# Instance normalization on one core: engine programs of its own with a loop on the chip, and the last tile in two halves

## The chip, the core and the metric

The kernel runs on one core of a Trainium2 chip. The metric is the device time of one execution in microseconds (us), lower is better. A kernel is run several times and the median is quoted. The profile is one execution taken by the hardware profiler; its span is some 1.7 us shorter than the time quoted. Engine names: PE multiplies matrices, DVE is the vector engine, ACT the scalar engine, POOL is GpSimd, SP issues the loads.

## The reference, cut to what matters

```python
# x: (8, 64, 32, 64, 64) float32, so 512 instances of 131,072 numbers
mean = np.mean(x, axis=(2, 3, 4), keepdims=True)
var = np.var(x, axis=(2, 3, 4), keepdims=True)
return ((x - mean) / np.sqrt(var + eps)).astype(np.float32)
```

Every number is read once and written once: 268.4 MB each way, 536.9 MB in all. There are two passes of arithmetic over each instance before its first number can be written.

## The kernel before

A tile is 128 partitions by 8,192 numbers (4 MB) and holds 8 instances of 16 partitions each; there are 64 tiles in six buffers. The framework of the kernel (its tile pools and scheduler) places all semaphores and waits, and the 64 tiles are written out one after the other in the program of each engine.

```python
avg = singles.tile([P, P], fp32, name="avg")     # 1/n_elem in 16 x 16 blocks: sums over an instance's partitions
...
def load(g):
    t = data_pool.tile([P, F], fp32, name="xt")  # one of six slots
    nc.sync.dma_start(out=t, in_=x_t[g])
    return t

def compute(t):
    cut = F // 2
    sums = stat_pool.tile([P, 2], fp32, name="sums")
    nc.vector.reduce_sum(out=sums[:, 0:1], in_=t[:, :cut], ...)                        # L83
    nc.scalar.activation(out=unused[:, cut:], in_=t[:, cut:], func=Act.Identity,
                         accum_out=sums[:, 1:2])                                       # L86
    nc.tensor.matmul(out=mean_ps, lhsT=avg, rhs=sums, ...)
    nc.vector.tensor_reduce(out=neg_mean, in_=mean_ps, op=Alu.add, negate=True, ...)
    nc.scalar.activation(out=unused, in_=t, func=Act.Square, bias=neg_mean,
                         accum_out=squares)                                            # L103
    nc.tensor.matmul(out=var_ps, lhsT=avg, rhs=squares, ...)
    ...   # std, 1/std, bias: four small instructions
    nc.vector.tensor_scalar(out=t[:, cut:], in0=t[:, cut:], scalar1=scale, scalar2=bias, ...)   # L114
    nc.scalar.activation(out=t[:, :cut], in_=t[:, :cut], func=Act.Identity,
                         scale=scale, bias=bias)                                       # L122

for g in range(n_tiles):
    t = load(g)
    compute(t)
    nc.scalar.dma_start(out=out_t[g], in_=t)                                           # L131
```

Of the kernel before, what the change touches and what calls it, by code (L numbers as in the profile page):

```python
# [1 line left out]

# [4 lines left out]


@with_exitstack
def kernel(  # L10
    ctx: ExitStack,
    tc: tile.TileContext,
    x: bass.AP,
    eps: bass.AP,
    out: bass.AP,
):
    nc = tc.nc
    fp32 = mybir.dt.float32
    Alu = mybir.AluOpType
    Act = mybir.ActivationFunctionType  # L20

    P = 128
    B, C, D, H, W = x.shape
    n_inst = B * C
    n_elem = D * H * W
    eps_f = float(eps)

    SPLIT = 16
    IPT = P // SPLIT
    F = n_elem // SPLIT  # L30
    n_tiles = n_inst // IPT
    SLOTS = 6

    x_t = x.rearrange("b c d h w -> (b c) (d h w)").rearrange(
        "(k i) (s f) -> k (i s) f", i=IPT, s=SPLIT
    )
    out_t = out.rearrange("b c d h w -> (b c) (d h w)").rearrange(
        "(k i) (s f) -> k (i s) f", i=IPT, s=SPLIT
    )

    singles = ctx.enter_context(tc.tile_pool(name="singles", bufs=1))
    data_pool = ctx.enter_context(tc.tile_pool(name="data", bufs=SLOTS))
    stat_pool = ctx.enter_context(tc.tile_pool(name="stats", bufs=4))
    psum_pool = ctx.enter_context(
        tc.tile_pool(name="psum", bufs=2, space=bass.MemoryType.PSUM)
    )


    avg = singles.tile([P, P], fp32, name="avg")
    nc.vector.memset(avg, 1.0 / n_elem)  # L50
    nc.gpsimd.affine_select(  # L51
        out=avg,
        in_=avg,
        pattern=[[-SPLIT, IPT], [0, SPLIT]],
        compare_op=Alu.is_ge,
        fill=0.0,
        base=0,
        channel_multiplier=1,
    )
    nc.gpsimd.affine_select(  # L60
        out=avg,
        in_=avg,
        pattern=[[SPLIT, IPT], [0, SPLIT]],
        compare_op=Alu.is_ge,
        fill=0.0,
        base=SPLIT - 1,
        channel_multiplier=-1,
    )

    eps_t = singles.tile([P, 1], fp32, name="eps_t")  # L70
    nc.vector.memset(eps_t, eps_f)  # L71

    unused = singles.tile([P, F], mybir.dt.uint8, name="unused")

    def load(g):
        t = data_pool.tile([P, F], fp32, name="xt")
        nc.sync.dma_start(out=t, in_=x_t[g])
        return t

    def compute(t):  # L80
        cut = F // 2
        sums = stat_pool.tile([P, 2], fp32, name="sums")
        nc.vector.reduce_sum(  # L83
            out=sums[:, 0:1], in_=t[:, :cut], axis=mybir.AxisListType.X
        )
        nc.scalar.activation(  # L86
            out=unused[:, cut:],
            in_=t[:, cut:],
            func=Act.Identity,
            accum_out=sums[:, 1:2],  # L90
        )
        mean_ps = psum_pool.tile([P, 2], fp32, name="mean_ps")
        nc.tensor.matmul(out=mean_ps, lhsT=avg, rhs=sums, start=True, stop=True)  # L93
        neg_mean = stat_pool.tile([P, 1], fp32, name="neg_mean")
        nc.vector.tensor_reduce(  # L95
            out=neg_mean,
            in_=mean_ps,
            axis=mybir.AxisListType.X,
            op=Alu.add,
            negate=True,  # L100
        )
        squares = stat_pool.tile([P, 1], fp32, name="squares")
        nc.scalar.activation(  # L103
            out=unused, in_=t, func=Act.Square, bias=neg_mean, accum_out=squares
        )
        var_ps = psum_pool.tile([P, 1], fp32, name="var_ps")
        nc.tensor.matmul(out=var_ps, lhsT=avg, rhs=squares, start=True, stop=True)  # L107
        std = stat_pool.tile([P, 1], fp32, name="std")
        nc.scalar.activation(out=std, in_=var_ps, func=Act.Sqrt, bias=eps_t)  # L109
        scale = stat_pool.tile([P, 1], fp32, name="scale")  # L110
        nc.vector.reciprocal(out=scale, in_=std)  # L111
        bias = stat_pool.tile([P, 1], fp32, name="bias")
        nc.vector.tensor_mul(out=bias, in0=neg_mean, in1=scale)  # L113
        nc.vector.tensor_scalar(  # L114
            out=t[:, cut:],
            in0=t[:, cut:],
            scalar1=scale,
            scalar2=bias,
            op0=Alu.mult,
            op1=Alu.add,  # L120
        )
        nc.scalar.activation(  # L122
            out=t[:, :cut], in_=t[:, :cut], func=Act.Identity, scale=scale, bias=bias
        )


    with tc.manual_schedule():
        for g in range(n_tiles):
            t = load(g)
            compute(t)  # L130
            nc.scalar.dma_start(out=out_t[g], in_=t)  # L131


# [1 line left out]
_INS = ['x', 'eps']  # L135
_OUTS = [((8, 64, 32, 64, 64), 'float32')]

_NUMBERS = {'eps': 9.999999747378752e-06}


# [26 lines left out]
```

## Time and profile before

| | before |
|---|---|
| time, median of 3 | 1249.35 us (1249.16 to 1250.83) |
| busy: ACT, DVE, PE | 77%, 37%, 6% |
| packets of the load queue and the store queue, share of 16 DMA engines | 49.9% and 49.8% |
| traffic | 430 GB/s |

From the page of the kernel before: the span, each engine's busy time, the DMA row of the 40 slices (busy tenths), and the table of DMA queues (packets, MB, the time of their packets as a share of 16 engines over the span).

```profile
span 1247.6 us, 1828 instructions
PE 73.6 (6%) x256; PEld 64.2 (5%) x256; DVE 467.4 (37%) x322; ACT 961.6 (77%) x386; POOL 0.9 (0%) x6
DMA  9999999999999999999999999999999999999998
...
q1 hardware_dynamic: 9216, 268.44, 49.9%
q10 hardware_dynamic: 9216, 268.44, 49.8%
q14 instruction: 9, 0.07, 0.0%
q8 instruction: 2, 0.03, 0.0%
```

The two data queues together take 99.7% of what 16 DMA engines have, so the DMA bounds the whole span. The two queues of kind "instruction" are easy to pass over, at 0.0%: they bring the program itself.

From the timeline of the kernel before, the last tile (start, duration, engine, line, operation, tiles; in brackets the idle time before it and what ended that):

```profile
1215.30 3.62 ACT L86 ACTIVATE unused<-xt 128x4096 uint8<-128x4096 f32 x1 [1.61 <-DMA xt<-in_x_dram]
...
1220.72 7.12 ACT L103 ACTIVATE unused<-xt,neg_mean 128x8192 uint8<-128x8192 f32 x1 [1.71 <-DVE neg_mean L95]
...
1229.35 3.80 ACT L122 ACTIVATE xt<-xt,bias,scale 128x4096 f32<-128x4096 f32 x1 [0.47 <-DVE bias L113]
1233.18 0.34 ACTq L131 DMA_DIRECT2D out_dram<-xt  x1
```

The last load is there at 1215.3 us, and its store is issued 17.9 us later. It looks as if this stretch stood open, but two earlier stores are still in the queue: the DMA packets show the 16 engines idle for only 0.8 us on average around 1233 us.

### The profile page before, as it was taken

What the parts mean: (1) busy time and instruction counts of PE and PEld (TensorE: products, weight loads), DVE (VectorE), ACT (ScalarE), POOL (GpSimd) and SP (SyncE); (2) the same over time, 40 slices, a digit from 0 to 9 for tenths busy, and PEclk for the clock granted to TensorE, in tenths of its full rate; (3) what the DMA queues carried; (4) which work ended last, traced back from release to release, by engine and by line L of the source; (5) the groups of instructions that cost most, each with busy time, mean ns of one, the idle gap of its engine ahead of it and who ended that gap; (6) DMA issues with size and microseconds to landing.
All of it is one profiled execution on the core that took longest, in us unless ns stands there. A gap on an engine that the chain in (4) does not pass through costs nothing.

```text
span 1247.6 us, 1828 instructions
## 1 busy us (share of the span) xinstructions
PE 73.6 (6%) x256; PEld 64.2 (5%) x256; DVE 467.4 (37%) x322; ACT 961.6 (77%) x386; POOL 0.9 (0%) x6
## 2 busy tenths in 40 slices
PE   0000000000000000000000000000000000000000
PEld 0000000000000000000000000000000000000000
DVE  2344433433334334343343433434334333343331
ACT  5888888787777877778777777777787777877774
POOL 0000000000000000000000000000000000000000
DMA  9999999999999999999999999999999999999998
GB/s 403 420 437 434 434 427 436 435 435 427 435 436 434 434 428 435 435 434 427 437 435 434 433 429 437 435 432 427 437 436 434 429 431 435 436 434 425 437 436 364
DMA packets 18443, 536.99 MB, mean 430 GB/s; under 512 B 2048, under 2 KB 2048, under 8 KB 2048
## 3 DMA queue, kind: packets, MB, share of 16 engines
q1 hardware_dynamic: 9216, 268.44, 49.9%
q10 hardware_dynamic: 9216, 268.44, 49.8%
q14 instruction: 9, 0.07, 0.0%
q8 instruction: 2, 0.03, 0.0%
HBM read 268.44 MB, written 268.44 MB: 430 GB/s over the span
## 4 chain that ended last, share of the span: by engine, by line
ACT 45%; DVE 32%; another core or an unknown queue 12%; PE 6%; issue 2%; DMA 1%; ACTq 0%
ACT unused L103 37%; DVE sums L83 19%; DVE xt L114 10%; ACT xt L122 4%; ACT unused L86 3%; PE var_ps L107 3%; PE mean_ps L93 3%; ACT std L109 1%; DMA xt<-in_x_dram 1%; DVE scale L111 1%; DVE neg_mean L95 1%; DVE bias L113 1%; ACTq L131 0%; ACT L109 0%
## 5 line engine op out<-in xcount | busy, mean ns | idle before, releaser
L103 ACT ACTIVATE unused<-xt,neg_mean 128x8192 uint8<-128x8192 f32 x64 | 455.8, 7121 | 100.6 <-DVE neg_mean L95 100.6
L83 DVE TENSOR_REDUCE sums<-xt 128x1 f32<-128x4096 f32 x64 | 282.8, 4419 | 167.6 <-DMA xt<-in_x_dram 167.6
L86 ACT ACTIVATE unused<-xt 128x4096 uint8<-128x4096 f32 x64 | 231.5, 3617 | 96.1 <-DMA xt<-in_x_dram 91.5
L122 ACT ACTIVATE xt<-xt,bias,scale 128x4096 f32<-128x4096 f32 x64 | 243.3, 3801 | 31.3 <-DVE bias L113 31.3
L111 DVE RECIPROCAL scale<-std 128x1 f32<-128x1 f32 x64 | 10.5, 164 | 530.8 <-ACT std L109 530.8
L114 DVE TENSOR_SCALAR xt<-xt,scale,bias 128x4096 f32<-128x4096 f32 x64 | 154.4, 2413 | 2.7 <-DVE bias L113 0.3
L93 PE MATMUL mean_ps<-sums,avg 128*128 128x2 f32 x128 | 36.0, 351 | 670.9 <-DVE sums L83 573.9
L93 PEld LDWEIGHTS mean_ps<-sums,avg 128*128 128x128 f32 x128 | 32.1, 311 | 674.7 <-ACT unused L86 657.1
L107 PE MATMUL var_ps<-squares,avg 128*128 128x1 f32 x128 | 37.6, 363 | 484.1 <-ACT unused L103 484.1
L107 PEld LDWEIGHTS var_ps<-squares,avg 128*128 128x128 f32 x128 | 32.1, 312 | 489.6 <-ACT unused L103 489.6
L109 ACT ACTIVATE std<-var_ps,eps_t 128x1 f32<-128x1 f32 x64 | 16.7, 261 | 42.7 <-PE var_ps L107 42.7
L95 DVE TENSOR_REDUCE neg_mean<-mean_ps 128x1 f32<-128x2 f32 x64 | 10.2, 160 | 60.1 <-PE mean_ps L93 60.1
L103 ACT ACTIVATION_READ_ACCUMULATOR unused<-xt,neg_mean 128x1 f32 x64 | 11.9, 187 | 0.0
L86 ACT ACTIVATION_READ_ACCUMULATOR unused<-xt 128x1 f32 x64 | 11.9, 186 | 0.0
L113 DVE TENSOR_TENSOR bias<-neg_mean,scale 128x1 f32<-128x1 f32 x64 | 10.2, 160 | 2.2
L86 ACT ACT_TABLE_LOAD x1 | 1.3, 1283 | 0.8 <-PEq L148 0.8
L109 ACT ACT_TABLE_LOAD x1 | 1.3, 1283 | 0.0
L50 DVE MEMSET avg<- 128x128 f32 x1 | 0.2, 165 | 0.9 <-PEq L148 0.9
L51 POOL TENSOR_SCALAR_AFFINE_SELECT avg<-avg 128x128 f32<-128x128 f32 x1 | 0.3, 343 | 0.6 <-DVE eps_t L71 0.6
L60 POOL TENSOR_SCALAR_AFFINE_SELECT avg<-avg 128x128 f32<-128x128 f32 x1 | 0.3, 338 | 0.1
L148 POOL MEMSET const-bfloat16-1.0<- 128x1 bf16 x1 | 0.1, 102 | 0.0
L148 POOL MEMSET const-uint8-127<- 128x1 uint8 x1 | 0.1, 102 | 0.0
(3 smaller groups left out, 0.3 us busy)
## 6 DMA issues: line engine op xcount, KB each, us to landing
xt<-in_x_dram SPq DMA_DIRECT2D x64, 4096.0 KB, 53.3
out_dram<-xt ACTq DMA_DIRECT2D x64, 4096.0 KB, 45.2
```

Source lines behind the costliest of these rows:

```text
L51: nc.gpsimd.affine_select(out=avg, in_=avg, pattern=[[-SPLIT, IPT], [0, SPLIT]], compare_op=Alu.is_ge, fill=0.0, base=0, channel_multiplier=1,
L83: nc.vector.reduce_sum(out=sums[:, 0:1], in_=t[:, :cut], axis=mybir.AxisListType.X)
L86: nc.scalar.activation(out=unused[:, cut:], in_=t[:, cut:], func=Act.Identity, accum_out=sums[:, 1:2],)
L93: nc.tensor.matmul(out=mean_ps, lhsT=avg, rhs=sums, start=True, stop=True)
L95: nc.vector.tensor_reduce(out=neg_mean, in_=mean_ps, axis=mybir.AxisListType.X, op=Alu.add, negate=True,)
L103: nc.scalar.activation(out=unused, in_=t, func=Act.Square, bias=neg_mean, accum_out=squares)
L107: nc.tensor.matmul(out=var_ps, lhsT=avg, rhs=squares, start=True, stop=True)
L109: nc.scalar.activation(out=std, in_=var_ps, func=Act.Sqrt, bias=eps_t)
L111: nc.vector.reciprocal(out=scale, in_=std)
L113: nc.vector.tensor_mul(out=bias, in0=neg_mean, in1=scale)
L114: nc.vector.tensor_scalar(out=t[:, cut:], in0=t[:, cut:], scalar1=scale, scalar2=bias, op0=Alu.mult, op1=Alu.add,)
L122: nc.scalar.activation(out=t[:, :cut], in_=t[:, :cut], func=Act.Identity, scale=scale, bias=bias)
```

## The change

Its intent: replace the framework's scheduling by a program for each engine with semaphores of its own, one set for each slot; put the tiles in a loop on the chip, six to a round, with waits against registers that count up; and cut the last tile in two halves, so that the work after the last load is shorter. The core of the diff, with cuts marked:

```diff
-    with tc.manual_schedule():
-        for g in range(n_tiles):
-            t = load(g)
-            compute(t)
-            nc.scalar.dma_start(out=out_t[g], in_=t)
+    slots = [sbuf(f"slot{s}", [P, COLS]) for s in range(SLOTS)]          # six, as before
+    landed = semaphores("landed", LANES)                                 # and ten more sets
...
+    def on_vector(eng, t, lane, n, c1, c2, c16):
+        eng.reduce_sum(out=a[:, 0:1], in_=t[:, :w], ...
+        )._wait_ge(landed[lane], c16).then_inc(summed[lane], 1)
...  # on_scalar, on_tensor: the same arithmetic and the same split as before
+    rest = [ ... tiles 60 to 62 ... ]
+    for h in range(2):                                                   # last tile: two halves
+        k = 2 * (n_tiles - 1) + h
+        half = slots[last][:, h * COLS // 2 : (h + 1) * COLS // 2]
+        rest.append((x_h[k], out_h[k], half, SLOTS + h, 1, FULL // 2))
...
+        with eng.Fori(0, ROUNDS) as it:                                  # ten rounds on the chip
+            for s in range(SLOTS):
+                step(eng, slots[s][:], s, FULL, *counts, *more)
+            for c, m in zip(counts, (1, 2, 16)):
+                eng.reg_add(c, c, m)
+        for _, dst, t, lane, c, n in rest:
+            step(eng, t, lane, n, c, 2 * c, 16 * c, *more)
...
+    @block.sync
+        with eng.Fori(1, ROUNDS) as it:
+            for s in range(SLOTS):
+                eng.dma_start(out=slots[s][:], in_=x_t[it * SLOTS + s])._wait_ge(
+                    stored[s], c16).then_inc(landed[s], 16)
```

A half of the last tile is 128 partitions by 4,096 numbers, so its rows are 16 KB where those of all other tiles are 32 KB.

More of the change, by code (lines that the diff above doesn't have):

```diff
@@ L26 @@
     eps_f = float(eps)
-    SPLIT = 16
-    IPT = P // SPLIT
-    F = n_elem // SPLIT
-    n_tiles = n_inst // IPT
+    COLS = 8192
     SLOTS = 6
-    x_t = x.rearrange("b c d h w -> (b c) (d h w)").rearrange(
-        "(k i) (s f) -> k (i s) f", i=IPT, s=SPLIT
-    )
-    out_t = out.rearrange("b c d h w -> (b c) (d h w)").rearrange(
-        "(k i) (s f) -> k (i s) f", i=IPT, s=SPLIT
-    )
-    singles = ctx.enter_context(tc.tile_pool(name="singles", bufs=1))
-    data_pool = ctx.enter_context(tc.tile_pool(name="data", bufs=SLOTS))
@@ L43 @@
-    stat_pool = ctx.enter_context(tc.tile_pool(name="stats", bufs=4))
-    psum_pool = ctx.enter_context(
-        tc.tile_pool(name="psum", bufs=2, space=bass.MemoryType.PSUM)
-    )
-    avg = singles.tile([P, P], fp32, name="avg")
-    nc.vector.memset(avg, 1.0 / n_elem)
-    nc.gpsimd.affine_select(
-        out=avg,
-        in_=avg,
-        pattern=[[-SPLIT, IPT], [0, SPLIT]],
-        compare_op=Alu.is_ge,
-        fill=0.0,
-        base=0,
-        channel_multiplier=1,
-    )
-    nc.gpsimd.affine_select(
-        out=avg,
-        in_=avg,
-        pattern=[[SPLIT, IPT], [0, SPLIT]],
-        compare_op=Alu.is_ge,
-        fill=0.0,
-        base=SPLIT - 1,
-        channel_multiplier=-1,
-    )
@@ L70 @@
-    eps_t = singles.tile([P, 1], fp32, name="eps_t")
-    nc.vector.memset(eps_t, eps_f)
-    unused = singles.tile([P, F], mybir.dt.uint8, name="unused")
-    def load(g):
-        t = data_pool.tile([P, F], fp32, name="xt")
-        nc.sync.dma_start(out=t, in_=x_t[g])
-        return t
-    def compute(t):
-        cut = F // 2
-        sums = stat_pool.tile([P, 2], fp32, name="sums")
-        nc.vector.reduce_sum(
-            out=sums[:, 0:1], in_=t[:, :cut], axis=mybir.AxisListType.X
-        )
-        nc.scalar.activation(
-            out=unused[:, cut:],
-            in_=t[:, cut:],
-            func=Act.Identity,
-            accum_out=sums[:, 1:2],
-        )
-        mean_ps = psum_pool.tile([P, 2], fp32, name="mean_ps")
-        nc.tensor.matmul(out=mean_ps, lhsT=avg, rhs=sums, start=True, stop=True)
-        neg_mean = stat_pool.tile([P, 1], fp32, name="neg_mean")
-        nc.vector.tensor_reduce(
-            out=neg_mean,
-            in_=mean_ps,
+    FULL = P * COLS // n_elem
@@ new lines @@
+    n_tiles = n_inst // FULL
+    ROUNDS = (n_tiles - 1) // SLOTS
+    LANES = SLOTS + 2
+    x_f = x.rearrange("b c d h w -> (b c) (d h w)")
+    out_f = out.rearrange("b c d h w -> (b c) (d h w)")
+    x_t = x_f.rearrange("(k i) (s f) -> k (i s) f", i=FULL, s=P // FULL)
+    out_t = out_f.rearrange("(k i) (s f) -> k (i s) f", i=FULL, s=P // FULL)
+    x_h = x_f.rearrange("(k i) (s f) -> k (i s) f", i=FULL // 2, s=2 * P // FULL)
+    out_h = out_f.rearrange("(k i) (s f) -> k (i s) f", i=FULL // 2, s=2 * P // FULL)
@@ new lines, with sbuf @@
+    ctx.enter_context(tc.tile_critical(name="norm"))
+    def sbuf(name, shape, dtype=fp32):
+        return ctx.enter_context(nc.sbuf_tensor(name, shape, dtype))
+    slots = [sbuf(f"slot{s}", [P, COLS]) for s in range(SLOTS)]
+    unused = sbuf("unused", [P, COLS], mybir.dt.uint8)
+    eps_t = sbuf("eps_t", [P, 1])
+    avg = {n: sbuf(f"avg{n}", [P, P]) for n in (FULL, FULL // 2)}
+    small = [sbuf(f"small{i}", [P, 8]) for i in range(LANES)]
+    psum = [
+        ctx.enter_context(nc.psum_tensor(f"psum{i}", [P, 512], fp32))
+        for i in range(LANES)
+    ]
@@ new lines, in semaphores @@
+    def semaphores(name, n):
+        return [ctx.enter_context(nc.semaphore(f"{name}{i}")) for i in range(n)]
+    ready = semaphores("ready", 1)[0]
+    landed = semaphores("landed", LANES)
+    summed = semaphores("summed", LANES)
+    meaned = semaphores("meaned", LANES)
+    centred = semaphores("centred", LANES)
+    squared = semaphores("squared", LANES)
+    varied = semaphores("varied", LANES)
+    rooted = semaphores("rooted", LANES)
+    scaled = semaphores("scaled", LANES)
+    shifted = semaphores("shifted", LANES)
@@ L98, in compute @@
+    done = semaphores("done", LANES)
+    stored = semaphores("stored", LANES)
+    def on_vector(eng, t, lane, n, c1, c2, c16):
+        w = t.shape[1] // 2
+        a = small[lane]
+        eng.reduce_sum(
+            out=a[:, 0:1], in_=t[:, :w], axis=mybir.AxisListType.X
+        )._wait_ge(landed[lane], c16).then_inc(summed[lane], 1)
+        eng.tensor_reduce(
+            out=a[:, 2:3],
+            in_=psum[lane][:, 0:2],
             axis=mybir.AxisListType.X,
@@ L100, in compute @@
             negate=True,
-        )
-        squares = stat_pool.tile([P, 1], fp32, name="squares")
-        nc.scalar.activation(
-            out=unused, in_=t, func=Act.Square, bias=neg_mean, accum_out=squares
-        )
-        var_ps = psum_pool.tile([P, 1], fp32, name="var_ps")
-        nc.tensor.matmul(out=var_ps, lhsT=avg, rhs=squares, start=True, stop=True)
-        std = stat_pool.tile([P, 1], fp32, name="std")
-        nc.scalar.activation(out=std, in_=var_ps, func=Act.Sqrt, bias=eps_t)
@@ L110, in compute @@
-        scale = stat_pool.tile([P, 1], fp32, name="scale")
-        nc.vector.reciprocal(out=scale, in_=std)
-        bias = stat_pool.tile([P, 1], fp32, name="bias")
-        nc.vector.tensor_mul(out=bias, in0=neg_mean, in1=scale)
-        nc.vector.tensor_scalar(
-            out=t[:, cut:],
-            in0=t[:, cut:],
-            scalar1=scale,
-            scalar2=bias,
+        )._wait_ge(meaned[lane], c1).then_inc(centred[lane], 1)
+        eng.reciprocal(out=a[:, 5:6], in_=a[:, 4:5])._wait_ge(
+            rooted[lane], c1
+        ).then_inc(scaled[lane], 1)
@@ L119, in compute @@
+        eng.tensor_mul(out=a[:, 6:7], in0=a[:, 2:3], in1=a[:, 5:6])._wait_ge(
+            scaled[lane], c1
+        ).then_inc(shifted[lane], 1)
+        eng.tensor_scalar(
+            out=t[:, w:],
+            in0=t[:, w:],
+            scalar1=a[:, 5:6],
+            scalar2=a[:, 6:7],
             op0=Alu.mult,
             op1=Alu.add,
-        )
-        nc.scalar.activation(
-            out=t[:, :cut], in_=t[:, :cut], func=Act.Identity, scale=scale, bias=bias
-        )
-    with tc.manual_schedule():
-        for g in range(n_tiles):
-            t = load(g)
-            compute(t)
-            nc.scalar.dma_start(out=out_t[g], in_=t)
+        )._wait_ge(shifted[lane], c1).then_inc(done[lane], 1)
@@ new lines, in on_scalar @@
+    def on_scalar(eng, t, lane, n, c1, c2, c16, dst):
+        w = t.shape[1] // 2
+        a = small[lane]
+        eng.activation(
+            out=unused[:, w : 2 * w],
+            in_=t[:, w:],
+            func=Act.Identity,
+            accum_out=a[:, 1:2],
+        )._wait_ge(landed[lane], c16).then_inc(summed[lane], 1)
+        eng.activation(
+            out=unused[:, : 2 * w],
+            in_=t,
+            func=Act.Square,
+            bias=a[:, 2:3],
+            accum_out=a[:, 3:4],
+        )._wait_ge(centred[lane], c1).then_inc(squared[lane], 1)
+        eng.activation(
+            out=a[:, 4:5], in_=psum[lane][:, 2:3], func=Act.Sqrt, bias=eps_t[:, 0:1]
+        )._wait_ge(varied[lane], c1).then_inc(rooted[lane], 1)
+        eng.activation(
+            out=t[:, :w],
+            in_=t[:, :w],
+            func=Act.Identity,
+            scale=a[:, 5:6],
+            bias=a[:, 6:7],
+        )._wait_ge(shifted[lane], c1).then_inc(done[lane], 1)
+        eng.dma_start(out=dst, in_=t)._wait_ge(done[lane], c2).then_inc(
+            stored[lane], 16
+        )
@@ new lines, in on_tensor @@
+    def on_tensor(eng, t, lane, n, c1, c2, c16):
+        a = small[lane]
+        eng.matmul(
+            out=psum[lane][:, 0:2],
+            lhsT=avg[n][:],
+            rhs=a[:, 0:2],
+            start=True,
+            stop=True,
+        )._wait_ge(summed[lane], c2).then_inc(meaned[lane], 1)
+        eng.matmul(
+            out=psum[lane][:, 2:3],
+            lhsT=avg[n][:],
+            rhs=a[:, 3:4],
+            start=True,
+            stop=True,
+        )._wait_ge(squared[lane], c1).then_inc(varied[lane], 1)
@@ new lines, with over_tiles @@
+    rest = [
+        (x_t[k], out_t[k], slots[k % SLOTS][:], k % SLOTS, k // SLOTS + 1, FULL)
+        for k in range(ROUNDS * SLOTS, n_tiles - 1)
+    ]
+    last = (n_tiles - 1) % SLOTS
+    for h in range(2):
+        k = 2 * (n_tiles - 1) + h
+        half = slots[last][:, h * COLS // 2 : (h + 1) * COLS // 2]
+        rest.append((x_h[k], out_h[k], half, SLOTS + h, 1, FULL // 2))
+    def over_tiles(eng, step, with_target=False):
+        counts = [
+            ctx.enter_context(eng.register(f"{step.__name__}_c{m}")) for m in (1, 2, 16)
+        ]
+        for c, m in zip(counts, (1, 2, 16)):
+            eng.reg_mov(c, m)
+        with eng.Fori(0, ROUNDS) as it:
+            for s in range(SLOTS):
+                more = (out_t[it * SLOTS + s],) if with_target else ()
+                step(eng, slots[s][:], s, FULL, *counts, *more)
+            for c, m in zip(counts, (1, 2, 16)):
+                eng.reg_add(c, c, m)
+        for _, dst, t, lane, c, n in rest:
+            more = (dst,) if with_target else ()
+            step(eng, t, lane, n, c, 2 * c, 16 * c, *more)
@@ new lines, with _ @@
+    block = ctx.enter_context(nc.Block())
+    @block.sync
+    def _(eng):
+        for s in range(SLOTS):
+            eng.dma_start(out=slots[s][:], in_=x_t[s]).then_inc(landed[s], 16)
+        c16 = ctx.enter_context(eng.register("load_c16"))
+        eng.reg_mov(c16, 16)
+        with eng.Fori(1, ROUNDS) as it:
+            for s in range(SLOTS):
+                eng.dma_start(out=slots[s][:], in_=x_t[it * SLOTS + s])._wait_ge(
+                    stored[s], c16
+                ).then_inc(landed[s], 16)
+            eng.reg_add(c16, c16, 16)
+        for src, _, t, lane, c, n in rest:
+            behind = lane if lane < SLOTS else last
+            uses = c - 1 if lane < SLOTS else ROUNDS
+            eng.dma_start(out=t, in_=src)._wait_ge(stored[behind], 16 * uses).then_inc(
+                landed[lane], 16
+            )
@@ new lines, in _ @@
+    @block.gpsimd
+    def _(eng):
+        count = 0
+        for n, m in avg.items():
+            split = P // n
+            eng.memset(m[:], 1.0 / n_elem).then_inc(ready, 1)
+            count += 1
+            for sign in (-1, 1):
+                eng.affine_select(
+                    out=m[:],
+                    in_=m[:],
+                    pattern=[[sign * split, n], [0, split]],
+                    compare_op=Alu.is_ge,
+                    fill=0.0,
+                    base=0 if sign < 0 else split - 1,
+                    channel_multiplier=-sign,
+                )._wait_ge(ready, count).then_inc(ready, 1)
+                count += 1
+        eng.memset(eps_t[:], eps_f).then_inc(ready, 1)
@@ new lines, with _ @@
+    READY = 3 * len(avg) + 1
+    @block.vector
+    def _(eng):
+        over_tiles(eng, on_vector)
+    @block.tensor
+    def _(eng):
+        eng.wait_ge(ready, READY)
+        over_tiles(eng, on_tensor)
+    @block.scalar
+    def _(eng):
+        eng.wait_ge(ready, READY)
+        over_tiles(eng, on_scalar, with_target=True)
+        for s in range(SLOTS):
+            uses = ROUNDS + sum(1 for r in rest if r[3] == s)
+            eng.wait_ge(stored[s], 16 * uses)
+        for s in range(SLOTS, LANES):
+            eng.wait_ge(stored[s], 16)
```

## The prediction

> What bounds the kernel now. The DMA engines do, over the whole span. In the profile's table of DMA queues the load queue's packets take 49.9% of 16 engines' span and the store queue's 49.8%: 99.7% of 1247.6 us, or 1243.9 us, leaving about 4 us in all. The row of slices says the same: DMA 9 in every slice but the last (8), 430 GB/s on average, 425 to 437 from slice to slice. The trace has 16,384 packets of 32 KB of 1.214 us each, which is 1,024 rounds of 16 engines. The Trainium skill ("DMA: Bandwidth & Descriptors", section "Where 436 GB/s comes from") puts the ceiling at 435 GB/s; this trace sits at it, so faster packets are not to be expected, and 536.87 MB must still move.
>
> ACT is busy 77%. A tile costs it 17.5 us where loads are ahead (between the passes that start at 36.66, 54.15 and 71.64 us in the chain of waits), while tiles come every 19.4 us (1201.27 to 1220.72), the time of 8.39 MB at 432 GB/s. So there are about 1.9 us of slack per tile. The chain names ACT (45%) and DVE (32%) only because it follows work through each tile; each step ends in a wait of 3.0 us for a load.
>
> What the change moves. Arithmetic, number of slots (six), transfer size, both queues and the order of loads and stores stay, except for the last tile.
> - Own programs, semaphores, loop: about 64 groups of waits become waits against registers, with an address computation before each looped DMA and a branch per round. I estimate under 0.5 us of ACT per tile, below its slack.
> - The build shows two activation table loads in the ACT loop's body, where the kernel before ran two in all. At 1.28 us each (timeline) that is about 2.6 us per round of six tiles, 26 us of ACT in all, against 6 x 1.9 = 11 us of slack a round. Visible in the trace, worth nothing in time.
> - Loads still wait for the store of the tile six before. Time to landing is 53 us for loads and 45 us for stores, so both queues hold more than two tiles of backlog; a hiccup of a few us on ACT or SP starves neither.
> - Last tile in halves: its load lands at 1215.3 and its store is issued at 1233.2, 17.9 us later. That looks like an exposed tail, but two stores are still queued then (about 9.7 us each alone); the DMA packets show idleness of only about 0.8 us averaged over 16 engines around 1233, and some 1.5 us of stragglers at the end. Halves remove the 0.8 and perhaps half of the stragglers; ACT finishes no earlier (two halves cost about 10 us each by my estimate from the pass durations), but the last store is 2 MB. Gain about 1 us.
> - Start and end: the first load still starts about 1 us in; barriers may cost or save under 1 us.
>
> On the critical path: about 1 us of about 1249. Predicted 1248.5 us, 80% range 1245.5 to 1252. Faster by over 2%: 0.01; within 2%: 0.98; slower by over 2%: 0.01.
>
> What would show it: DMA queues together again 99.5% or more; looped transfers 4096 KB, load to landing about 53 us; some 20 table loads on ACT and ACT busy about 80%; the last store issued near 1234 us with DMA busy through it; instructions fewer in the program but not in the trace.
>
> What would make it wrong: looped DMAs with computed addresses split into smaller packets; ACT over 19.4 us a tile through slow register waits, branches or refetch after the branch, so that the queues run dry; a queue order that lets the stores fall behind.

## The result, and the profile after

The changed kernel takes 1248.36 us (median of 4, 1248.32 to 1248.60) against 1249.38 us (median of 4) for the kernel before. The ratio is 0.999, with a 95% interval of 0.9972 to 1.0007. The time is within 0.2 us of the predicted 1248.5.

The same lines of the changed kernel's page, with its two groups of table loads and the DMA issues of its loads (KB each, median us from issue to landing):

```profile
span 1246.9 us, 1819 instructions
PE 76.4 (6%) x260; PEld 65.2 (5%) x260; DVE 467.9 (38%) x325; ACT 986.1 (79%) x410; POOL 1.9 (0%) x11
...
q1 hardware_dynamic: 9360, 268.44, 50.0%
q10 hardware_dynamic: 9360, 268.44, 49.9%
q14 instruction: 3, 0.02, 0.0%
...
L107 ACT ACT_TABLE_LOAD x10 | 12.8, 1283 | 10.4 <-ACT slot L123 7.1
L120 ACT ACT_TABLE_LOAD x10 | 12.8, 1283 | 0.2
...
slot<-in_x_dram SPq DMA_DIRECT2D x63, 4096.0 KB, 52.8
slot<-in_x_dram SPq DMA_DIRECT2D x2, 2048.0 KB, 55.6
```

The DMA is as full as before, there are 20 table loads as the build had shown, and transfers and latencies are those of before. What is new are two things that I had not looked for: the packets that bring the program fell from 11 to 3 (one of the 3 has only 24 bytes, so 2 are pieces of the program), and the loads of the halves, of half the size, took longer to land than whole tiles. The timeline of the changed kernel's last tile:

```profile
1212.38 1.91 ACT L107 ACTIVATE unused<-slot 128x2048 uint8<-128x2048 f32 x1 [0.42 <-ACT slot L123]
...
1222.55 0.34 ACTq L130 DMA_DIRECT2D out_dram<-slot  x1
1223.47 1.91 ACT L107 ACTIVATE unused<-slot 128x2048 uint8<-128x2048 f32 x1 [0.96 <-DMA slot<-in_x_dram]
...
1233.92 0.34 ACTq L130 DMA_DIRECT2D out_dram<-slot  x1
```

The second half is there at 1223.5 us, 8 us later than the whole tile of the kernel before, and the last store is issued 0.7 us later than before. It is half as large, and the last landing comes at 1245.35 us against 1246.81. Of these 1.5 us, 0.7 are given back at the exit: from the last landing to the end of the span it is 1.55 us, where the kernel before has 0.83. So the size fits, but is it the halves that gained the 1.5 us, as I had said?

### The profile page after: what moved, and what is told of

It reads as the page before. It is cut to its first block, busy times and chain, and to the rows that moved or that the text cites. A ratio compares the mean times of both kernels' runs of the same rounds, so it can differ in the third digit from the quotient of the medians.

```text
span 1246.9 us, 1819 instructions
## 1 busy us (share of the span) xinstructions
PE 76.4 (6%) x260; PEld 65.2 (5%) x260; DVE 467.9 (38%) x325; ACT 986.1 (79%) x410; POOL 1.9 (0%) x11
## 4 chain that ended last, share of the span: by engine, by line
ACT 48%; DVE 29%; another core or an unknown queue 13%; PE 6%; issue 1%; DMA 1%; ACTq 0%; DVEq 0%; SPq 0%
ACT unused L113 37%; DVE small L79 18%; DVE slot L95 8%; ACT slot L123 4%; ACT unused L107 4%; PE psum L136 3%; PE psum L143 3%; ACT small L120 1%; ACT L120 1%; DMA slot<-in_x_dram 1%; DVE small L89 1%; DVE small L82 1%; DVE small L92 1%; ACTq L130 0%
## 5 line engine op out<-in xcount | busy, mean ns | idle before, releaser
L113 ACT ACTIVATE unused<-slot,small 128x8192 uint8<-128x8192 f32 (+1 forms) x65 | 456.1, 7017 | 90.1 <-DVE small L82 90.1
L79 DVE TENSOR_REDUCE small<-slot 128x1 f32<-128x4096 f32 (+1 forms) x65 | 282.9, 4353 | 164.4 <-DMA slot<-in_x_dram 164.4
L107 ACT ACTIVATE unused<-slot 128x4096 uint8<-128x4096 f32 (+1 forms) x65 | 231.7, 3564 | 82.1 <-DMA slot<-in_x_dram 77.0
L123 ACT ACTIVATE slot<-slot,small 128x4096 f32<-128x4096 f32 (+1 forms) x65 | 243.7, 3749 | 27.6 <-DVE small L92 27.6
L95 DVE TENSOR_SCALAR slot<-slot,small 128x4096 f32<-128x4096 f32 (+1 forms) x65 | 154.7, 2379 | 2.4
L136 PE MATMUL psum<-small,avg 128*128 128x2 f32 x130 | 38.2, 363 | 674.1 <-DVE small L79 548.7
L136 PEld LDWEIGHTS psum<-small,avg 128*128 128x128 f32 x130 | 32.6, 311 | 679.6 <-DVE small L79 553.0
L143 PE MATMUL psum<-small,avg 128*128 128x1 f32 x130 | 38.2, 363 | 480.6 <-ACT unused L113 480.6
L143 PEld LDWEIGHTS psum<-small,avg 128*128 128x128 f32 x130 | 32.7, 312 | 486.2 <-ACT unused L113 486.2
L120 ACT ACTIVATE small<-psum,eps_t 128x1 f32<-128x1 f32 x65 | 17.0, 261 | 37.4 <-PE psum L143 37.3
L107 ACT ACT_TABLE_LOAD x10 | 12.8, 1283 | 10.4 <-ACT slot L123 7.1
L120 ACT ACT_TABLE_LOAD x10 | 12.8, 1283 | 0.2
L107 ACT ACTIVATION_READ_ACCUMULATOR unused<-slot 128x1 f32 x65 | 12.1, 186 | 0.0
```

The costliest lines, as they stand in the source:

```text
L79: eng.reduce_sum(out=a[:, 0:1], in_=t[:, :w], axis=mybir.AxisListType.X)._wait_ge(landed[lane], c16).then_inc(summed[lane], 1)
L95: eng.tensor_scalar(out=t[:, w:], in0=t[:, w:], scalar1=a[:, 5:6], scalar2=a[:, 6:7], op0=Alu.mult, op1=Alu.add,)._wait_ge(shifted[lane], ...
L107: eng.activation(out=unused[:, w : 2 * w], in_=t[:, w:], func=Act.Identity, accum_out=a[:, 1:2],)._wait_ge(landed[lane], c16).then_inc(sum ...
L113: eng.activation(out=unused[:, : 2 * w], in_=t, func=Act.Square, bias=a[:, 2:3], accum_out=a[:, 3:4],)._wait_ge(centred[lane], c1).then_in ...
L120: eng.activation(out=a[:, 4:5], in_=psum[lane][:, 2:3], func=Act.Sqrt, bias=eps_t[:, 0:1])._wait_ge(varied[lane], c1).then_inc(rooted[lane ...
L123: eng.activation(out=t[:, :w], in_=t[:, :w], func=Act.Identity, scale=a[:, 5:6], bias=a[:, 6:7],)._wait_ge(shifted[lane], c1).then_inc(don ...
```

## The experiments

Every experiment gave correct results. They ran on three chips (e1 to e4, e5 to e8, e9 to e12), each set beside the kernel before, whose medians there were 1249.25, 1249.47 and 1249.36 us; a difference between sets of 0.2 us says nothing. The first four take the change apart: loop or no loop, halves or whole, own programs or the framework's.

**e1: the changed kernel again**, as the yardstick on the same chip.

> The changed kernel itself, as the yardstick for the three kernels beside it. Both theories: 1248.3 to 1248.6 us, some 1.0 us under the kernel before (1249.4), since the DMA engines are busy 99.7% of either span.

Measured: 1248.52 us (1248.28 to 1248.56), beside 1249.25 for the kernel before.

**e2: the changed kernel with the last tile whole.**

```diff
-        for k in range(ROUNDS * SLOTS, n_tiles - 1)
+        for k in range(ROUNDS * SLOTS, n_tiles)
     ]
-    for h in range(2):
-        ...
-        rest.append((x_h[k], out_h[k], half, SLOTS + h, 1, FULL // 2))
```

> The changed kernel with its last tile in one piece again; own programs, semaphores and loop stay. Theory (the gain is the halves, and the own programs give some back at the exit): the last store starts late again and the DMA idles some 0.8 us before it, so 1249.8 to 1250.4 us, above the kernel before (1249.4), because about 0.7 us more lies between the last landing and the end (0.8 us in the kernel before, 1.5 us in the changed one). Rival (the gain is the own programs with fewer waits and the loop): 1248.3 to 1248.6 us, as the whole change.

Measured: 1248.35 us (1248.25 to 1248.65). My theory falls: without the halves the whole gain is still there. The longer exit is there as I said (1.68 us after the last landing), yet the DMA engines have no idle gap before the last store any more, although that store is whole. The last load landed some 2 us earlier than in the kernel before, as the timeline of e2 shows (compare 1215.30 and 1233.18 before):

```profile
1213.41 3.62 ACT L107 ACTIVATE unused<-slot 128x4096 uint8<-128x4096 f32 x1 [1.72 <-DMA slot<-in_x_dram]
...
1231.12 0.34 ACTq L130 DMA_DIRECT2D out_dram<-slot  x1
```

**e3: the changed kernel with the loop written out**, constants in place of registers; halves and semaphores stay.

```diff
-        with eng.Fori(0, ROUNDS) as it:
+        for it in range(ROUNDS):
+            counts = [m * (it + 1) for m in (1, 2, 16)]
             for s in range(SLOTS):
```

> The changed kernel with the loop written out and constants in place of the registers; halves and semaphores stay. Theory (the loop lies in ACT's slack): same as the changed kernel within 0.3 us, 1248.1 to 1248.7 us, although ACT's table loads fall from 20 to 2 and its busy time by some 23 us. Rival (the loop costs time that the rest gains back): ACT's 23 us show at least in part, 1240 to 1247 us.

Measured: 1249.27 us (1249.14 to 1249.50). Neither: ACT lost its 18 extra table loads and the kernel got slower, by 0.75 us beside e1, on the same chip. No run of e3 lies within the runs of e1 or e2. So the loop gains and the 23 us of table loads cost nothing. From the page of e3 (with the loop ACT had 986.1 us in 410 instructions, and the instruction queue 3 packets):

```profile
PE 76.4 (6%) x260; PEld 65.3 (5%) x260; DVE 468.2 (38%) x325; ACT 963.0 (77%) x392; POOL 1.9 (0%) x11
...
q14 instruction: 7, 0.06, 0.0%
q8 instruction: 2, 0.03, 0.0%
```

**e4: the kernel before with only its last tile in halves.**

```diff
+        t = data_pool.tile([P, F], fp32, name="xt")
+        halves = [(2 * n_tiles - 2 + h, t[:, h * F // 2 : (h + 1) * F // 2]) for h in range(2)]
+        for k, half in halves:
+            nc.sync.dma_start(out=half, in_=x_h[k])
+        for k, half in halves:
+            compute(half, avg_h, F // 2)
+            nc.scalar.dma_start(out=out_h[k], in_=half)
```

> The kernel before with only its last tile in two halves; its scheduler's waits stay, no loop. Theory: it has the whole gain of the halves (1.6 us less at the last DMA packet) without the longer exit, 1247.6 to 1248.2 us, below both kernels. Rival (own programs and loop gain): 1249.2 to 1249.5 us, as the kernel before.

Measured: 1256.92 us (1256.72 to 1261.75), 7.7 us slower than before, which no theory had. Its trace shows ACT waiting once, for 21.4 us, near the end of the stream. e7 and e8 are about this.

**A new theory.** The trace has each packet that brings a piece of the program, with its time and size: 8 KB packets of 0.31 us and 16 KB packets of 0.92 to 0.96 us. They run on the same DMA engines as the data. The trace does not number the engines, but it shows the collisions: in e6 (below), between 40 and 1190 us, each of the 8 fetches has one 32 KB data packet that starts within 1.3 us of it and takes 1.46 to 1.75 us instead of 1.213, and no other data packet takes over 1.31 us. In the kernel before it is the same, 11 of 11. The Trainium skill ("DMA: Bandwidth & Descriptors", section "Queues, rings and completion order") says that row 14 of the queues is internal to the runtime, and the traces agree that a queue 14 exists which no instruction of the kernel issues on. A tile is spread evenly over 16 engines, and each has no time left over (99.7%), so, by this theory, an engine that must carry such a packet stays behind for the rest of the run, and each tile lands with the engine that is furthest behind. The trace lets one see this, because a transfer raises its semaphore 16 times; the same page (section "Why a DMA increments its semaphore by 16 and not by 1") explains that each engine used does so for its own share. I take the "lag" of a landing as the last of its 16 increments minus the eighth. This is worked out from the semaphore times of e6, below, which has no loop and no halves, around the packets of its instruction queues:

```
start of packet, size        lag of the landing before   lag of the second landing after
158.6 and 170.8 us, 8 KB each    0.17 us                     0.87 us
416.5 us, 16 KB                  0.79                        1.44
660.5 us, 8 KB                   1.32                        1.71
1155.1 us, 8 KB                  1.60                        2.34
```

The lag stands nearly still between such packets and jumps by 0.35 to 0.75 us at each of them. (Four packets, at 499.2, 848.3, 1036.1 and 1216.7 us, have no such jump; presumably they hit engines that were not the last one.) The trace of e3 has the same jumps at the same packets, and a lag of 2.46 us at its last load. At the landing of the last load it is 3.80 us in the kernel before (11 packets in the stream), 2.35 in e6 (9), 1.97 in the changed kernel (2; 1.72 in e1, the same kernel) and 1.70 in e2 (1).

The packets are not the whole of the lag. In e2 nearly all of the 1.70 us is a steady drift, of about 0.03 us a tile from 250 us on, with no packet beside it; at its last loads 15 of the 16 engines are within 0.5 us and one alone is late. In the kernel before the lag of the loads steps up beside the packets, from 0.15 to 1.81 us at 536 us, and then drifts by about 0.06 us a tile to 3.80, with no step at the last six packets. In e2 the drift can be seen in the packets too: 129 of those of 32 KB between 120 and 1190 us take 4 to 100 ns more than 1213 ns, 1.4 us in all. e6 has such packets as well (1.2 us in all), but there, it seems, the last engines are those that the fetches hit. What causes the drift stays open.

**e5: more fetches.** e2 plus 2,560 memsets on the idle GpSimd, each of one byte in every partition and each to its own place; nobody waits for them.

```diff
+    spare = sbuf("spare", [P, 2560], mybir.dt.uint8)
...
+        for i in range(2560):
+            eng.memset(spare[:, i : i + 1], 0)
```

> The looped kernel with its last tile whole (1248.35 us), plus 2,560 one-element memsets on the idle GpSimd that nobody waits for. New theory (the loop's gain is fewer instruction fetches: each is an 8 KB packet of 0.31 us on one of the 16 DMA engines that carry the data, and the tile, and the kernel, end with the engine that is furthest behind): some 20 more packets on the instruction queue, all on one engine, 20 x 0.31 = 6.2 us behind the others; the kernel ends 4 to 6.5 us later, 1252.4 to 1254.9 us. Rival (fetches are harmless, the 0.9 us between looped and written-out programs lies in branches, waits or table loads): 1248.2 to 1248.7 us, unchanged.

Measured: 1261.43 us (1258.95 to 1265.37), 13 us more. The page counts the packets:

```profile
q1 hardware_dynamic: 9216, 268.44, 49.4%
q10 hardware_dynamic: 9216, 268.44, 49.2%
q14 instruction: 21, 0.17, 0.0%
```

The direction is that of the theory and the size is twice the expected. The lag is 14.9 us at 122 us, just after the memsets (the last one starts at 114.5 us), and it never comes back: it goes on growing, without further packets of program, to 15.6 us at 297 us and 21.2 us at the last load. (The profiled run is the slowest of the five.) It also opened a gap at the end: the queue ran dry before the last store, because the last load landed so late.

**e9: a quarter of it**, 640 memsets.

> As e5, with 640 memsets in place of 2,560: some 5 more fetches, the number that one engine of the kernel before carried. New theory: each fetch sets one DMA engine back by about 0.6 us (e5: 13 us for 20, about twice the 0.31 us that the fetch itself takes), so some 3 us there by the end, less what that engine had in hand: 1249.8 to 1251.8 us. Rival (in e5 it was GpSimd's own work beside the others, not the fetches): 640 memsets are over within 35 us, so 1248.2 to 1249.0 us.

Measured: 1261.75 us (1256.6 to 1265.01); 6 packets of program in the profiled run, which is one of the two fastest. Far too much for five packets, by either account. The lag is 3.2 us at 35 us, when the memsets are over (the last one ends at 28.4 us), 6.2 us at 55, and then the lag of the loads grows by about 0.1 us a tile to 12.4 us, with a single further packet of program (at 106 us). **So five packets do not explain this run**, and its runs scatter over 8 us, where most kernels have all runs but one within 1 us.

**e10: the same 2,560 memsets in a loop** on GpSimd, which keeps the program small.

```diff
-        for i in range(2560):
-            eng.memset(spare[:, i : i + 1], 0)
+        with eng.Fori(0, 160) as it:
+            for i in range(16):
+                eng.memset(spare[:, bass.ds(it * 16 + i, 1)], 0)
```

> As e5, the same 2,560 memsets on GpSimd, but written as a loop of 160 rounds of 16, so that the program stays small. New theory (fetches cost, not GpSimd's work): 1 to 4 fetches in the stream and 1248.2 to 1249.5 us. Rival (GpSimd's memsets disturb the others): 1255 to 1265 us, as e5.

Measured: 1254.10 us (1253.93 to 1254.21), between what the two theories said. With a single packet of program the lag still grows, from 0.2 us at 50 us to 6.0 us at 288 us, which is when the last memset runs, and then nearly stops (7.2 at the end). So the work on GpSimd by itself sets a DMA engine back (of the 16 increments of the last load, 15 come within 1.5 us and the last one 6.5 us after them), by about 5.8 us / 2,560 = 2.3 ns a memset, and my control was not clean: e5 and e9 have both causes. An estimate for e5 from the two: 20 packets of 0.35 us and 2,560 memsets of 2.3 ns are 7.0 + 5.8 = 12.8 us, near its 14.9 us of lag right after the memsets; for e9 at 35 us, 5 x 0.35 + 640 x 2.3 ns = 3.2 us, as measured, but not its growth later. How a memset comes to delay a DMA engine, and why e5 and e9 drift on, no trace here shows; nor does any run separate the memsets from the profiler's recording of them.

What the three do show together is the part that matters for the argument: a delay of a few us on one of the 16 engines, caused by something off to the side that no chain of waits names, was not made up in any of these runs and comes out at the end in good part (e10: 5.5 us more lag at the last load than e2, 5.75 us more time).

**e6: no loop, last tile whole**, the fourth corner (both edits above).

> Own programs and semaphores, no loop, last tile whole: the fourth corner beside the looped kernels with halves (1248.5) and whole (1248.35) and the written-out one with halves (1249.27). New theory (the number of instruction fetches decides, halves are worth nothing): 1249.0 to 1249.5 us, with 9 or 10 fetches during the stream. Rival (halves are worth about 1 us where nothing else hides it): 1250.0 to 1250.5 us.

Measured: 1249.00 us (1248.79 to 1249.88). Its page has these queues, against `q14 instruction: 2` and no q8 in e2:

```profile
q14 instruction: 7, 0.06, 0.0%
q8 instruction: 2, 0.03, 0.0%
```

| | loop | no loop |
|---|---|---|
| halves | 1248.36, 1248.52 us (2 fetches in the stream) | 1249.27 us (9) |
| whole | 1248.35 us (1) | 1249.00 us (9) |

Down the columns halves are worth nothing (if anything, 0.2 us less than nothing). Along the rows the loop is worth 0.65 to 0.9 us. The 95% intervals of the ratios are some 0.1% wide on either side and include 1 for all four, so this rests on two other things: no run of a looped kernel of this table is as long as any run of a written-out one (at most 1248.65 against at least 1248.79 us), and the traces. The first is firm for the row of halves (e1 and e3, one chip). In the row of whole tiles e2 and e6 ran on different chips; against the kernel before on its own chip e2 gained 0.90 us and e6 0.47, which leaves 0.43 for the loop. And the kernel before, which is written out, had single runs of 1248.47 and 1248.83 us among its 35. The trace of e6 beside e2 has the steps: the lag is 0.65 us greater (2.35 against 1.70), the last landing comes 0.8 us later (1245.68 against 1244.91), and the span ends 0.8 us later (1247.4 against 1246.6). Beside the kernel before (1249.47 in these rounds) e6 also shows what own programs and semaphores are worth by themselves: at most 0.5 us. By its trace they do more than that at one end and lose it at the other: the last landing comes 1.1 us earlier than in the kernel before (1245.68 against 1246.81) and the exit takes 0.9 us more (1.72 against 0.83).

**e7: halves on the kernel before, but loaded by one transfer**, so that the number of loads is unchanged.

```diff
-        for k, half in halves:
-            nc.sync.dma_start(out=half, in_=x_h[k])
+        nc.sync.dma_start(out=t.rearrange("p (h f) -> p h f", h=2),
+                          in_=x_h[k : k + 2].rearrange("h p f -> p h f"))
```

> The kernel before with its last tile computed and stored in halves, but loaded by one transfer, so that the count of loads stays 64. New theory (run e4 lost 7.6 us because its 65th load shifted the order in which loads and stores share eight semaphores, so that a store had to wait 21 us for a load): no such wait of ACT, and 1248.8 to 1249.6 us, as the kernel before, since halves are worth nothing and the fetches are as before. Rival (halves themselves cost the 7.6 us, by more work on ACT at the end): 1255 to 1257 us. The theory of my prediction: about 1248 us.

Measured: 1253.72 us (1253.62 to 1253.82). A miss of 4 us. The long wait of e4 is gone, as expected, but another one is there, at the end, in the timeline of e7:

```profile
1213.37 0.34 ACTq L133 DMA_DIRECT2D out_dram<-xt  x1
1223.43 1.91 ACT L88 ACTIVATE unused<-xt 128x2048 uint8<-128x2048 f32 x1 [10.09 <-DMA xt<-in_x_dram]
```

The last load lands 8 us later than the same bytes do in the kernel before. Its packets are 16 KB, and it competes with stores of 32 KB packets. From the changed kernel's trace, the packets that started between 1193 and 1212 us, while a half was loading:

```
load   178 packets of 16 KB, 2.92 MB
store  160 packets of 32 KB, 5.24 MB
```

By packets the load has about half, by bytes a third. In the kernel before the same stretch has 119 packets of load and 128 of store, all of 32 KB. The Trainium skill ("DMA: Bandwidth & Descriptors", section "Queues, rings and completion order") says that each DMA engine "round-robins between the queue rows it has work for, at *packet* granularity", and the counts agree. So does the order: where one can follow an engine's packets, each starting as the one before it ends, rows of load and store alternate. (The page gives a packet as some 9 to 17 descriptors; here a turn is one contiguous row of 16 or 32 KB, which is what the trace lists as one packet. How many descriptors that is, the trace does not say.)

**e8: the kernel before with its last load as two transfers**, everything else unchanged.

```diff
+            nc.sync.dma_start(out=t[:, : F // 2], in_=x_t[g][:, : F // 2])
+            nc.sync.dma_start(out=t[:, F // 2 :], in_=x_t[g][:, F // 2 :])
```

> The kernel before with nothing changed but its last load issued as two transfers of half the columns; last tile computed and stored whole. New theory (the shifted semaphores): the same wait of some 20 us of ACT for a load appears near 1135 us and the kernel takes 1254 to 1258 us. Rival (halves themselves cost it): 1249.0 to 1249.7 us.

Measured: 1258.52 us (1258.46 to 1264.78), just above the expected range. The wait of e4 is back, without any halves in the arithmetic:

```profile
1132.52 3.80 ACT L126 ACTIVATE xt<-xt,bias,scale 128x4096 f32<-128x4096 f32 x1 [0.49 <-DVE bias L117]
1157.33 0.34 ACTq L135 DMA_DIRECT2D out_dram<-xt  x1
1157.71 3.62 ACT L90 ACTIVATE unused<-xt 128x4096 uint8<-128x4096 f32 x1 [21.39 <-DMA xt<-in_x_dram]
```

ACT's data was ready at 1136.3 us, and its store went out at 1157.3. In the built programs of e4 and e8 loads and stores take turns on eight semaphores of the framework in the order in which they are written; one more load moves everything after it by one place, and from there on a store can have to wait for a load that shares its semaphore and is still under way. The trace of e8 shows this: the store that goes out at 1157.33 us raises the same semaphore as the load issued at 1104.55, waited for that semaphore, and that load landed at 1157.23. While it waits, it blocks ACT. A program with semaphores of its own for every slot, as the change has them, cannot meet this.

**e11: small packets alone.** e2 with its last load as two transfers of half the columns (16 KB rows), both counted on the slot's own semaphore; arithmetic and store whole.

```diff
+            for cols in (slice(0, COLS // 2), slice(COLS // 2, COLS)):
+                eng.dma_start(out=t[:, cols], in_=src[:, cols])._wait_ge(
+                    stored[behind], 16 * uses).then_inc(landed[lane], 16)
```

> The looped kernel with its last tile computed and stored whole, but loaded by two transfers of half the columns, so that its packets are 16 KB beside stores of 32 KB. Theory (the two queues take turns packet by packet, so a load of half-size packets gets a third of the rate in place of half; that is why halves gain nothing): the last load lands at 1221 to 1224 us instead of 1213.3, its store is issued near 1240 instead of 1231, the DMA runs dry for 5 to 8 us before it, 1252 to 1257 us. Rival (the packet size of one tile does not matter): 1248.2 to 1248.9 us.

Measured: 1255.53 us (1255.40 to 1255.77), as expected but for the idle time, which is a little longer. From its timeline:

```profile
1212.17 0.34 ACTq L130 DMA_DIRECT2D out_dram<-slot  x1
1223.58 3.62 ACT L107 ACTIVATE unused<-slot 128x4096 uint8<-128x4096 f32 x1 [11.44 <-DMA slot<-in_x_dram]
...
1241.28 0.34 ACTq L130 DMA_DIRECT2D out_dram<-slot  x1
```

The same bytes land 10 us later than in e2 (1223.6 against 1213.4), the last store goes out 10 us later, and the packets show the 16 engines idle for 8.6 us before it. So the packet size of a single tile, at the end, costs 7 us. (e11 also has one transfer more than e2; e7, with the same rows in one transfer, landed just as late, at 1223.4 us.) In the changed kernel this cost is there too, but the second half needs only 10.4 us of arithmetic in place of 17.7, and so its store is in the queue in time. The halves repay just what their own packets cost.

**e12: more work for ACT.** e2 with ACT summing 5,120 columns of the first pass and DVE 3,072.

```diff
-            out=a[:, 0:1], in_=t[:, :w], axis=mybir.AxisListType.X
+            out=a[:, 0:1], in_=t[:, : w - 1024], axis=mybir.AxisListType.X
...
-            in_=t[:, w:],
+            in_=t[:, w - 1024 :],
```

> The looped kernel, last tile whole, with the first pass's split moved so that ACT sums 5,120 columns and DVE 3,072 instead of 4,096 each: 0.85 us more of ACT a tile, 55 us in all. Theory (DMA bounds, a tile costs ACT 17.8 us of 19.4): 1248.2 to 1249.5 us. Rival (ACT, named by the chain with 48%, bounds): some 50 us longer.

Measured: 1248.92 us (1248.71 to 1248.95), 0.6 us above e2, which ran on another chip; its trace has a lag of 2.08 us at the last load, 0.38 more than e2, and its last landing is as much later. From its page:

```profile
PE 75.2 (6%) x256; PEld 64.2 (5%) x256; DVE 397.6 (32%) x320; ACT 1039.4 (83%) x404; POOL 1.9 (0%) x11
L107 ACT ACTIVATE unused<-slot 128x5120 uint8<-128x5120 f32 x64 | 286.1, 4470 | 61.9 <-DMA slot<-in_x_dram 52.6
```

About 55 us of work went onto the engine that the chain of waits names first, and the time moved by about one hundredth of that. This is what slack looks like.

## Why the prediction was right, point by point

The predicted time, 1248.5 us, was met within 0.2 us, and so was "same". "Same" was reasoned; the last microsecond was luck, for the reason given for it was wrong. The gain of the loop (and at most 0.5 us of the own programs), which I had put at nothing, stood in for the gain of the halves, which I had put at 1 us.

- **The DMA bounds, and the change cannot touch that**: right. The queues' shares are 99.9% after, and e12 confirms that ACT has room.
- **Loop, register waits and 20 table loads lie in ACT's slack**: right in that they cost nothing (e3, e6 against e1, e2). Wrong in that they were put down as worth nothing: the loop is worth 0.65 to 0.9 us between the medians (0.4 where the chips are allowed for, e6). The first step that failed is "Visible in the trace, worth nothing in time". I had read the table of DMA queues down to the third line, seen 0.0% for the instruction queues, and gone on. They carry little, but on engines that have nothing to spare, and a tile waits for the slowest of 16.
- **"Halves remove the 0.8 and perhaps half of the stragglers ... Gain about 1 us"**: wrong. This is the second step that failed. The idle gap of 0.8 us was real, and it is gone after the change, but in e2 it is gone without halves. The last load simply lands 2 us earlier there. What the halves do by themselves is to land later, because small packets get a smaller share (e7, e11), and to shorten the arithmetic by as much; the table of four corners puts their worth at zero or just below.
- **"ACT finishes no earlier"**: right; the last store is issued at 1233.92 against 1233.18.
- **"Start and end: ... barriers may cost or save under 1 us"**: right; the exit costs 0.7 us more (1.55 against 0.83).

The sum, from one trace each of the kernel before, of e6 (own programs, no loop) and of e2 (own programs and loop, no halves):

| | before | e6 | e2 |
|---|---|---|---|
| last landing, us | 1246.81 | 1245.68 | 1244.91 |
| from there to the end of the span, us | 0.83 | 1.72 | 1.68 |
| span, us | 1247.6 | 1247.4 | 1246.6 |
| lag at the last load, us | 3.80 | 2.35 | 1.70 |

So of the 1.9 us by which the last landing moved, 1.1 came with the own programs, which gave most of it back at the exit, and 0.8 with the loop, about as much as the lag fell by (0.65). That the fetches make the lag is shown for e6 and e3 by the steps at their times. In the kernel before they make less than half of it (at most 1.7 us of 3.80, by 536 us); the rest is the drift, whose cause is open, and why the own programs have less of it is open too. The dose of fetches (e5, e9) could not be separated from the side effect of GpSimd's own instructions (e10), so a price per fetch stays an estimate: about 0.35 us for 8 KB, from three such packets of e6 (a fourth, at 1155.1 us, cost 0.74).

No version beats both kernels clearly. e2, without the halves, equals the changed kernel (1248.35 against 1248.36 and 1248.52) and is simpler.

## What to carry to other kernels

When 16 DMA engines are full all the time, ask first whether a change moves bytes or packets; if it does not, expect nothing from it, and look at the end of the span for the rest. A tile lands with its slowest DMA engine, and in these runs what delayed one of them was not made up later: a long written-out program, whose pieces are fetched on those same engines, cost a little (under 1 us of 1249), and a loop on the chip took that away. Cutting the last piece smaller pays only if the DMA would otherwise stand idle, and its smaller packets lost out against larger ones of another queue (e7, e11), so cut it such that its rows stay as long as the others.

## What the Trainium skill lacked or had wrong

- "DMA: Bandwidth & Descriptors" says that rows of queues take turns by packet, but not what follows for two queues with rows of different length: here 178 packets of 16 KB against 160 of 32 KB in the same stretch, so about a third of the rate for the load, and 7 us for one tile (e11).
- The same page gives a packet as some 9 to 17 descriptors, but not as bytes or time; in these traces a turn is one row of 16 or 32 KB (1.213 us for 32 KB, 0.611 us for 16 KB, medians).
- On fetching the program, "Runtime: NRT & Kernel Launch" (section "Instruction fetch mechanics") calls the cost of crossing a block boundary "mostly hidden". It says nothing of what the fetches do to a stream that is bound by DMA: here 8 KB packets of 0.31 us and 16 KB packets of 0.92 to 0.96 us, at most of which a data packet on the same engine took 1.4 to 1.75 us instead of 1.213, and steps of 0.35 to 0.74 us in the lag (e6); 9 to 11 such packets in the written-out programs, 1 or 2 in the looped ones.
- No page that I found has that memsets on GpSimd, of one element per partition, set a DMA engine back: 5.8 us of lag for 2,560 of them (e10).
- The 435 GB/s that the section "Where 436 GB/s comes from" of "DMA: Bandwidth & Descriptors" gives as the ceiling of the fabric fit these traces: 420 to 437 GB/s from slice to slice before, between the first slice and the last. The same section says, and the prediction left out, that for transfers between HBM and SBUF the side of the HBM binds, at some 358 GB/s; here, with one core at work, such transfers ran at 430 GB/s.
